# Scale and shift of the first norm as columns: stationary weight blocks against two moving columns

## The chip, the cores and the metric

One core of a Trainium2 chip. The metric is the time of the device in microseconds, the median of several executions; the profile is of one further execution.

## The reference

One layer of a trunk over 1024 latent tokens (`x`, 1024 wide) and 256 context tokens (`ctx`). What matters here is its first step: a modulated RMSNorm of both streams, whose scale and shift are products of a conditioning vector with two of the six 1024-column parts of `w_mod`.

```python
cond = jax.nn.silu(c)
cond_ctx = jax.nn.silu(c_ctx)
mod = cond @ w_mod[l] + b_mod[l]
sh1, sc1, g1, sh2, sc2, g2 = jnp.split(mod[:, None, :], N_MOD, axis=-1)
mc = cond_ctx @ w_mod[l] + b_mod[l]
csh1, csc1, cg1, csh2, csc2, cg2 = jnp.split(mc, N_MOD, axis=-1)
hc = modulate(rmsnorm(ctx, norm1_g[l]), csh1, csc1)     # h * (1 + scale) + shift
hx = modulate(rmsnorm(x, norm1_g[l]), sh1, sc1)
proj = h @ w_in
```

Before the norm a fixed position code is added to `x`. After it come the input projection, a Fourier branch and a gated recurrent branch, the output projection, a second norm, a router, and 16 experts with a SwiGLU each (the longest stage), and a last norm.

## The kernel before

All in one program; `phase_a` is the part that the change touches. Tokens are held as tiles of 128 tokens by 1024 channels (`x0` to `x7`, and `cx0`, `cx1` for the context). For the projections they are turned around: `x_tr` transposes the 128x128 block `k` of four token tiles into one 128x512 tile (PSUM), `xnT`, channels on the partitions. `make_h(k, h, ..)` then applies scale and shift per channel (`s1`, `sh1`: 128 partitions, two columns for each `k`, one for latent and one for context tokens) and splits the result into a high and a low float32r part, `hTh` and `hTl`, half `h` being tokens 0 to 511 or 512 to 1023. `proj(k, n)` multiplies these with the split weights `wh`, `wl` by three float32r matmuls each (`mm3`), into the accumulators `pj`.

*Loads.* SyncE's queue issues them in program order: eight tiles of `wmod` part 1 (the scale, `wm1_0` to `wm1_7`, 128x1024, 512 KB each), `wm0_0` of part 0 (the shift), `x0` to `x3`, then the rest of part 0 with the input weights `wr4`, `wr5` (128x512) among them, then `x4` to `x7` and the context. `x4` to `x7` reuse the buffers of `wm1_0` to `wm1_5`.

*Scale and shift (L370 to L431).* The conditioning is the stationary operand, 4 columns wide, and the rows of `wmod` move past it, 512 columns at a time. For part 1 and for `wm0_5`, `wm0_6` each tile is split into float32r parts (`m_hi` on ScalarE, `m_lo` on VectorE, 1024 columns each) and multiplied by four matmuls (`m_pe`); the other tiles of part 0 (`m_f32`) go as float32, two matmuls, but the calls after the prologue loop split `wm0_4` too. The result is two rows of 4x512. `mod_end` copies them to `modrow`, turns them with eight small transposes (`modT`, L422) and adds the bias on VectorE.

*Tokens.* `x_in(j)` adds the position code: the right half by `colpos` (on GpSimd for the tiles in `XPG`, else on VectorE), the left half by `rp`, a small matmul. `x_sq` sums squares on ScalarE, `rstd` and `norm` follow.

*Order.* A scheduler places the instructions; what is pinned (`Pinned`, `pin`) keeps the order of the program on its engine. The calls from the line with `mod_mm(1, k)` to the loop over `k` that holds `make_h` are thus an order written by hand.

The rest of the program (phases c to f and `moe`) stays as it is in the source; there GpSimd's queue loads the trig tables and the remaining parts of `wmod` (`mraw`), and VectorE sums those (`macc`, L839).

## Time and profile before

| | |
|---|---|
| median of 3 runs | 1981.69 us (1981.35 to 1982.66) |
| profiled execution | 1983.2 us |
| its span | 1981.4 us |
| TensorE busy | 1899.9 us (96%) |
| VectorE busy | 1750.4 us (88%) |
| ScalarE busy | 1357.3 us (69%) |
| GpSimd busy | 137.0 us (7%) |

The span is the profiled program from its first to its last instruction; the execution's own time is 1.8 us longer. PE is TensorE's matmuls, PEld its weight loads, DVE VectorE, ACT ScalarE, POOL GpSimd, SP SyncE. A row of the timeline gives start, duration, engine, line, operation, what is written and read, the shapes and how many instructions are merged; in brackets the idle time ahead of it and who ended it. A float32 matmul that is no transpose shows as two records. PEclk is the granted clock of TensorE as a share of 2.4 GHz.

### The profile page before, as it was taken

How to read it: one execution, taken by the hardware profiler on the slowest of the kernel's cores; microseconds unless marked ns; L12 is line 12 of the kernel's file. 1: busy time of each engine (PE TensorE's matmuls, PEld its weight loads, DVE VectorE, ACT ScalarE, POOL GpSimd, SP SyncE). 2: the span in 40 equal slices, each digit the busy share in tenths (PEclk: the TensorE clock that was granted, in tenths of full speed). 3: DMA queues.
4: the chain of work that ended last, by engine and by line, in shares of the span. 5: the costliest groups of instructions: out<-in, count | busy, mean ns of one | idle time of the engine just before them, and what ended most of it. 6: DMA issues, size and time to landing. Idle time of an engine off the chain costs nothing.

```text
span 1981.4 us, 24505 instructions
## 1 busy us (share of the span) xinstructions
PE 1899.9 (96%) x9434; PEld 1559.9 (79%) x9434; DVE 1750.4 (88%) x1629; ACT 1357.3 (69%) x1094; POOL 137.0 (7%) x134
## 2 busy tenths in 40 slices
PE   7989889969999999999999999999999999999996
PEld 2777777857787888888888888888888888888885
DVE  7889787789998989898999999998989898989897
ACT  6567643346676777777777777777777777777775
POOL 2310101220002000000000000000000000000000
PEclk9999989979999999999999999999999999999998
DMA  8353554578999999999999999999999999999994
GB/s 330 112 159 123 191 173 149 207 285 334 350 357 339 379 368 390 381 386 367 388 363 391 355 406 364 396 366 381 379 381 375 384 381 376 385 375 387 366 390 178
DMA packets 113956, 651.34 MB, mean 329 GB/s; under 512 B 12743, under 2 KB 20472, under 8 KB 46254
## 3 DMA queue, kind: packets, MB, share of 16 engines
q1 hardware_dynamic: 100718, 602.55, 79.2%
q0 software_dynamic: 10816, 38.82, 6.9%
q10 hardware_dynamic: 2304, 8.39, 1.1%
q8 instruction: 74, 1.21, 0.2%
q14 instruction: 44, 0.36, 0.0%
HBM read 622.98 MB, written 26.74 MB: 328 GB/s over the span
## 4 chain that ended last, share of the span: by engine, by line
PE 76%; DVE 9%; DMA 6%; issue 5%; ACT 1%; POOL 1%; SPq 0%; POOLq 0%; DVEq 0%; ACTq 0%
PE gu L611 44%; PE y L611 22%; PE mx L611 4%; DVE lo L228 3%; DMA mraw<-in_wmod_dram 3%; PE ht L1627 2%; DMA x<-in_x_dram 1%; DVE macc L839 1%; PE xt L1498 1%; ACT hi L227 1%; DMA trr<-in_trig_dram 1%; PE hp L1185 1%; PE pq L611 1%; DVE g L716 0%; DVE r L714 0%
## 5 line engine op out<-in xcount | busy, mean ns | idle before, releaser
L228 DVE TENSOR_TENSOR lo<-raw,hi 128x2048 fp32r<-128x2048 f32 x525 | 1197.8, 2296 | 130.2 <-ACT hi L227 128.9
L227 ACT ACTIVATE hi<-raw 128x2048 fp32r<-128x2048 f32 x525 | 1006.9, 1918 | 311.2 <-PE gu L611 210.2
L611 PE MATMUL gu<-hi,xgh 128*128 128x512 f32 (+1 forms) x1536 | 580.0, 378 | 0.0
L611 PE MATMUL gu<-hi,xgl 128*128 128x512 f32 (+1 forms) x1536 | 572.9, 373 | 0.0
L611 PE MATMUL gu<-lo,xgh 128*128 128x512 f32 (+1 forms) x1536 | 572.2, 373 | 0.0
L611 PEld LDWEIGHTS gu<-hi,xgl 128*128 128x128 f32 x1536 | 290.2, 189 | 51.8 <-DVE xgl L228 0.2
L611 PEld LDWEIGHTS gu<-lo,xgh 128*128 128x128 f32 x1536 | 290.7, 189 | 49.0 <-issue 0.2
L611 PEld LDWEIGHTS gu<-hi,xgh 128*128 128x128 f32 x1536 | 290.5, 189 | 48.6 <-issue 0.2
L611 PE MATMUL y<-hi,hh 128*128 128x512 f32 x704 | 282.3, 401 | 0.0
L611 PE MATMUL y<-hi,hl 128*128 128x512 f32 x704 | 276.2, 392 | 1.4 <-DVE hl L228 1.4
L611 PE MATMUL y<-lo,hh 128*128 128x512 f32 x704 | 275.0, 391 | 0.0
L611 PEld LDWEIGHTS y<-hi,hl 128*128 128x128 f32 x704 | 132.5, 188 | 30.7 <-DVE hl L228 1.8
L611 PEld LDWEIGHTS y<-lo,hh 128*128 128x128 f32 x704 | 132.9, 189 | 25.5 <-issue 0.2
L611 PEld LDWEIGHTS y<-hi,hh 128*128 128x128 f32 x704 | 132.8, 189 | 25.0 <-issue 0.2
L1620 ACT ACTIVATE hid<-gu 128x512 f32<-128x512 f32 x96 | 54.1, 564 | 87.1 <-PE gu L611 87.1
L1637 POOL DMA_INDIRECT accx<-ys,idx x15 | 24.0, 1598 | 1014.2 <-DVE ys L1636 940.8
L228 DVE TENSOR_TENSOR hl<-ht,hh 128x512 fp32r<-128x512 f32 x96 | 61.4, 640 | 0.0
L1621 DVE TENSOR_TENSOR hid<-hid,gu 128x512 f32<-128x512 f32 x96 | 61.0, 636 | 0.0
L1627 PE MATMUL ht<-k_ident,hid 128*128 128x128 f32 x352 | 54.7, 274 | 5.3 <-DVE hid L1621 5.3
L1627 PEld LDWEIGHTS ht<-k_ident,hid 128*128 128x128 f32 x352 | 44.1, 141 | 19.2 <-DVE hid L1621 7.3
L839 DVE SCALAR_TENSOR_TENSOR macc<-mraw,cond,macc 128x512 f32<-128x512 f32 x56 | 41.8, 748 | 18.8 <-DMA mraw<-in_wmod_dram 18.1
L227 ACT ACTIVATE hh<-ht 128x512 fp32r<-128x512 f32 x96 | 52.0, 542 | 3.5 <-PE ht L1627 3.5
(434 smaller groups left out, 1819.6 us busy)
## 6 DMA issues: line engine op xcount, KB each, us to landing
raw<-in_wg_dram SPq DMA_DIRECT2D x160, 1024.0 KB, 7.1
raw<-in_wu_dram SPq DMA_DIRECT2D x160, 1024.0 KB, 7.3
raw<-in_wd_dram SPq DMA_DIRECT2D x160, 1024.0 KB, 7.1
raw<-in_wt_dram SPq DMA_DIRECT2D x32, 1024.0 KB, 7.7
mraw<-in_wmod_dram POOLq DMA_DIRECT2D x32, 512.0 KB, 4.7
raw<-in_wdt_dram SPq DMA_DIRECT2D x16, 1024.0 KB, 6.9
wm<-in_wmod_dram SPq DMA_DIRECT2D x16, 512.0 KB, 9.7
wr<-in_win_dram SPq DMA_DIRECT2D x24, 256.0 KB, 3.5
```

The costliest lines, as they stand in the source:

```text
L227: i = self.nc.scalar.activation(hi, src, AF.Copy)
L228: j = (eng or self.nc.vector).tensor_tensor(lo, src, hi, op=ALU.subtract)
L611: i = nc.tensor.matmul(out, l, r, start=st, stop=sp)
L839: nc.vector.scalar_tensor_tensor(acc, w[:, i], c, acc, op0=ALU.mult, op1=ALU.add)
L1185: self.pin(nc.tensor.matmul(q[:, 1024:1024 + E], hT[:, k], wr[:, k], start=k == 0, stop=k == KD - 1))
L1498: nc.tensor.transpose(p[:, 128 * i:128 * i + 128], xg[:, 128 * k:128 * k + 128], self.ident)
L1620: nc.scalar.activation(hid[:, 0:w], p[:, 0, 0:w], AF.Silu)
L1621: nc.vector.tensor_tensor(hid[:, 0:w], hid[:, 0:w], p[:, 1, 0:w], op=ALU.mult)
L1627: self.nc.tensor.transpose(q[:, c:c + 128], hid[:, c:c + 128], self.ident)
L1637: self.nc.gpsimd.indirect_dma_start(out=self.accx, out_offset=bass.IndirectOffsetOnAxis(ap=idx[:, :1], axis=0), in_=ys, in_offset=None, co ...
```

## The change

The products are turned around: each 128x128 block of a `wmod` tile becomes a stationary operand and the two columns of the conditioning (`condk`, float32) move past it, so a tile takes eight float32 matmuls and the result arrives as 128 partitions with two columns per block, `modp`, to which `mod_end` adds the bias straight from PSUM. The splits of `wmod`, `modrow`, `modT` and the 4-column forms go. The first four token tiles load before `wmod`. `hTh` is computed by ScalarE straight from the normed tile with scale and shift, not from `ht`. The low parts of the input weights (`w_split`) move from GpSimd to VectorE, two of them into the loop over `k`; `x_in(4)` to `x_in(7)` all move into that loop; `colpos` of `x0` to `x4` is added on VectorE, that of `x5` to `x7` on GpSimd.

```diff
--- before.py
+++ after.py
@@ -141,9 +141,7 @@
     return out
 
 
-XPG = (0, 2, 5, 6, 7)
 PL = ((2, 0), (5, 0))
-SPL = (5, 6)
 
 
 class Pinned:
@@ -311,18 +309,15 @@
             wm[m, k] = self.c5(f"wm{m}_{k}", (128, D), tag="lr" if k < 6 else "xs") if m else self.c4(f"wm{m}_{k}")
             nc.sync.dma_start(wm[m, k], a["wmod"][m, k])
 
+        for k in range(4):
+            load_x(k)
         for k in range(KD):
             load_m(1, k)
-        load_m(0, 0)
-        for k in range(4):
-            load_x(k)
-        for k in range(1, 5):
-            load_m(0, k)
         prefetch(4, 0)
         prefetch(5, 0)
+        for k in range(KD):
+            load_m(0, k)
         prefetch(4, 1)
-        for k in range(5, KD):
-            load_m(0, k)
         prefetch(5, 1, True)
         xn = [self.c4(f"xnT{k}", (128, 2, 512)) for k in range(4)]
         xn = [xn[k // 2][:, k % 2] for k in range(KD)]
@@ -355,17 +350,14 @@
         V.tensor_scalar(self.chalf, t[4], 0.5 * LRU_C, None, op0=ALU.mult)
 
         cond = self.small("cond", 16)
-        condk = self.small("condk", 32)
-        sg = condk[:, 0:16]
+        condk = self.small("condk", 16)
+        sg = self.small("sg", 16)
         nc.scalar.activation(sg, cols[:, 0:16], AF.Sigmoid)
         nc.vector.tensor_tensor(cond, sg, cols[:, 0:16], op=ALU.mult)
         self.cond = cond
         condv = cond.rearrange("p (v k) -> p k v", v=2)
-        condk = condk.rearrange("p (k v) -> p k v", v=4)
-        V.memset(condk[:, :, 2:4], 0.0)
-        V.tensor_copy(condk[:, :, 0:2], condv)
-        cr = self.small("condr", 32, F32R).rearrange("p (k v) -> p k v", v=4)
-        self.split(condv, cr[:, :, 0:2], cr[:, :, 2:4])
+        condk = condk.rearrange("p (k v) -> p k v", v=2)
+        V.tensor_copy(condk, condv)
 
         ss, rs = self.small("ss", 10), self.small("rs", 10)
         junk = self.pro.tile([128, D], F32, tag="mraw", name="junk", bufs=2)
@@ -375,56 +367,18 @@
         def tr(name, shape=(128, 512)):
             return self.ps.tile(list(shape), F32, tag="tr", name=name, bufs=4)
 
-        modp = {}
-        PV, PA, PG = (self.pinned(e) for e in (nc.vector, nc.scalar, nc.gpsimd))
-
-        wh, wl = {}, {}
-
-        def m_hi(m, k):
-            wh[m, k] = self.c4(f"wh{m}_{k}", dt=F32R)
-            PA.activation(wh[m, k], wm[m, k], AF.Copy)
-
-        def m_lo(m, k):
-            wl[m, k] = self.c4(f"wl{m}_{k}", dt=F32R)
-            PV.tensor_tensor(wl[m, k], wm[m, k], wh[m, k], op=ALU.subtract)
-
-        def m_pe(m, k):
-            if k == 0:
-                modp[m] = [self.ps.tile([128, 512], F32, tag="pj", name=f"modp{m}{h}", bufs=4) for h in range(2)]
-            for z, w in ((0, wh), (1, wl)):
-                for h in range(2):
-                    i = nc.tensor.matmul(modp[m][h][0:4], cr[:, k], w[m, k][:, 512 * h:512 * h + 512],
-                                         start=k + z == 0, stop=k + z == KD)
-                    self.pin(i)
-
-        def m_f32(m, k):
-            if k == 0:
-                modp[m] = [self.ps.tile([128, 512], F32, tag="pj", name=f"modp{m}{h}", bufs=4) for h in range(2)]
-            for h in range(2):
-                self.pin(nc.tensor.matmul(modp[m][h][0:4], condk[:, k], wm[m, k][:, 512 * h:512 * h + 512],
-                                          start=k == 0, stop=k == KD - 1))
+        PV, PA = (self.pinned(e) for e in (nc.vector, nc.scalar))
+        modp = {m: self.ps.tile([128, KD, 2], F32, tag="pj", name=f"modp{m}", bufs=4) for m in (1, 0)}
 
         def mod_mm(m, k):
-            if m == 0 and k not in SPL:
-                return m_f32(m, k)
-            m_hi(m, k)
-            m_lo(m, k)
-            m_pe(m, k)
+            for c in range(KD):
+                self.pin(nc.tensor.matmul(modp[m][:, c], wm[m, k][:, 128 * c:128 * c + 128], condk[:, k],
+                                          start=k + c == 0, stop=k == KD - 1, skip_group_check=True))
 
         def mod_end(m):
-            c = 4
-            row = self.pro.tile([c, 1024], F32, tag="mraw", name=f"modrow{m}", bufs=2)
-            PA.activation(row[:, 0:512], modp[m][0][0:c], AF.Copy)
-            PV.tensor_copy(row[:, 512:], modp[m][1][0:c])
-            yield
-            p = tr(f"modT{m}", (128, KD, c))
-            for k in range(KD):
-                self.pin(nc.tensor.transpose(p[:, k], row[:, 128 * k:128 * k + 128], self.ident[0:c, 0:c]))
-            yield
             dv = (s1 if m else sh1).rearrange("p (k v) -> p k v", v=2)
             b = cols[:, COL["bsc"]:COL["bsc"] + 8] if m else cols[:, COL["bsh"]:COL["bsh"] + 8]
-            PV.tensor_tensor(dv, p[:, :, 0:2], b[:, :, None].to_broadcast([128, 8, 2]), op=ALU.add)
-            PV.tensor_tensor(dv, dv, p[:, :, 2:4], op=ALU.add)
+            PV.tensor_tensor(dv, modp[m], b[:, :, None].to_broadcast([128, 8, 2]), op=ALU.add)
             if m:
                 g = cols[:, COL["n1g"]:COL["n1g"] + 8]
                 PV.scalar_tensor_tensor(dv, dv, 1.0, g[:, :, None].to_broadcast([128, 8, 2]),
@@ -439,7 +393,7 @@
 
         def x_in(j, sq=True):
             p = rp.pop(j) if j in rp else x_pos(j)
-            (PG if j in XPG else PV).tensor_tensor(x[j][:, 512:], x[j][:, 512:], colpos, op=ALU.add)
+            (nc.gpsimd if j > 4 else V).tensor_tensor(x[j][:, 512:], x[j][:, 512:], colpos, op=ALU.add)
             self.pin(V.tensor_tensor(x[j][:, :512], x[j][:, :512], p, op=ALU.add))
             if sq:
                 x_sq(j)
@@ -469,33 +423,24 @@
             s = slice(512 * h, 512 * h + 512)
             t = self.pr.tile([128, 512], F32, tag="ht", name=f"ht{k}{h}", bufs=2)
             sc, sh = s1[:, 2 * k:2 * k + 1], sh1[:, 2 * k:2 * k + 1]
+            nc.scalar.activation(self.hh[k][:, s], src, AF.Identity, scale=sc, bias=sh)
             if h and k % 2:
                 nc.scalar.activation(t, src, AF.Identity, scale=sc, bias=sh)
             else:
                 V.tensor_scalar(t, src, sc, sh, op0=ALU.mult, op1=ALU.add)
-            self.split(t, self.hh[k][:, s], self.hl[k][:, s], eng=nc.gpsimd if (k, h) in PL else None)
+            (nc.gpsimd if (k, h) in PL else V).tensor_tensor(self.hl[k][:, s], t, self.hh[k][:, s], op=ALU.subtract)
 
         nc.scalar.activation(self.small("warm", 8), cols[:, COL["n1g"]:COL["n1g"] + 8], AF.Sqrt)
         for j in range(4):
             rp[j] = x_pos(j)
-        for k in range(KD):
-            mod_mm(1, k)
-        mod_mm(0, 0)
         for k in range(4):
             x_in(k)
-            if k:
-                mod_mm(0, k)
         self.rstd(ss[:, 0:4], rs[:, 0:4], 1.0 / D, self.pr, 4)
         w = {}
-        end1, end0 = mod_end(1), mod_end(0)
 
         def w_split(q):
             t, h = q % 2, q // 2
-            w[t, h] = self._get_w(4 + t, h, self.wraw.pop((4 + t, h)), True, nc.gpsimd)
-
-        for j in range(4):
-            norm(x[j], j)
-        w_split(0)
+            w[t, h] = self._get_w(4 + t, h, self.wraw.pop((4 + t, h)), True)
 
         def xn_tr(*ks):
             for k in ks:
@@ -505,33 +450,22 @@
                 else:
                     PV.tensor_copy(xn[k], p)
 
-        def m_split(k):
-            m_hi(0, k)
-            m_lo(0, k)
-
-        m_split(4)
-        xn_tr(0, 1)
-        m_split(5)
-        next(end1)
-        xn_tr(2, 3)
-        m_pe(0, 4)
+        for j in range(4):
+            norm(x[j], j)
+        for k in range(KD):
+            mod_mm(1, k)
+            if k > 5:
+                xn_tr(2 * k - 12, 2 * k - 11)
+        mod_end(1)
+        mod_mm(0, 0)
+        xn_tr(4, 5)
+        w_split(0)
+        mod_mm(0, 1)
+        xn_tr(6, 7)
         w_split(1)
-        m_split(6)
-        xn_tr(4, 5)
-        next(end1)
-        m_pe(0, 5)
-        w_split(2)
-        next(end1, None)
-        xn_tr(6, 7)
-        m_pe(0, 6)
-        x_in(4, False)
-        w_split(3)
-        mod_mm(0, 7)
-        next(end0)
-        x_sq(4)
-        x_in(5, False)
-        for _ in end0:
-            pass
+        for k in range(2, KD):
+            mod_mm(0, k)
+        mod_end(0)
         pj = {(t, n): self.ps.tile([128, 512], F32, tag="pj", name=f"pj{t}{n}", bufs=4) for t in range(2) for n in range(2)}
 
         def proj(k, n):
@@ -541,14 +475,12 @@
                 self.mm3(pj[t, n], wh[:, k % 4], wl[:, k % 4], self.hh[k][:, s], self.hl[k][:, s], k == 0, k == KD - 1)
 
         for k in range(KD):
-            if k == 2:
-                self.pin(nc.gpsimd.tensor_copy(self.small("dm", 1), cx[1][:, 0:1]))
             make_h(k, 0, xn[k])
             proj(k, 0)
-            if k == 0:
-                x_sq(5)
             if k < 2:
-                x_in(6 + k)
+                w_split(2 + k)
+            if k < 4:
+                x_in(4 + k)
             if k == 4:
                 self.rstd(ss[:, 4:8], rs[:, 4:8], 1.0 / D, self.pr, 4)
                 for j in range(4, NT):
```

TensorE, from the last tile of the scale to the first projection. `wm1_7` is the eighth tile of part 1, `tr00` a transposed block, `rp4` a position matmul, `pj00` the first projection; `x8` is eight instructions. Before:

```order
L396 MATMUL modp10_213<-wh1_7_267,condr_191 4x512
L396 MATMUL modp11_214<-wh1_7_267,condr_191 4x512
L396 MATMUL modp10_213<-wl1_7_269,condr_191 4x512
L396 MATMUL modp11_214<-wl1_7_269,condr_191 4x512
L404 MATMUL modp00_275<-wm0_0_103,condk_186 4x512
L404 MATMUL modp01_276<-wm0_0_103,condk_186 4x512
...
L437 LDWEIGHTS sel48_80
L437 MATMUL rp4_410<-enc48_79,sel48_80 128x512
L404 MATMUL modp00_275<-wm0_7_131,condk_186 4x512
L404 MATMUL modp01_276<-wm0_7_131,condk_186 4x512
...
L422 MATMUL modT0_428<-k_ident_83,modrow0_420 128x4 x8
L611 MATMUL pj00_439<-hTh0_443,wh4_0_311 128x512
```

With the change:

```order
L375 MATMUL modp1_196<-condk_186,wm1_6_107 128x2 x8
L413 MATMUL tr00_290<-k_ident_83,x0_87 128x128
...
L413 MATMUL tr10_296<-k_ident_83,x3_93 128x128
L375 MATMUL modp1_196<-condk_186,wm1_7_109 128x2 x8
L413 MATMUL tr20_310<-k_ident_83,x0_87 128x128
...
L375 MATMUL modp0_197<-condk_186,wm0_0_115 128x2 x8
L413 MATMUL tr40_332<-k_ident_83,x0_87 128x128
...
L375 MATMUL modp0_197<-condk_186,wm0_2_119 128x2 x8
...
L375 MATMUL modp0_197<-condk_186,wm0_7_129 128x2 x8
L543 MATMUL pj00_421<-hTh0_425,wh4_0_344 128x512
```

Four 512-column matmuls per tile of the scale, and two per tile of the shift, have become eight 2-column ones; the transposes stand between the tiles' blocks, `rp4` has gone behind the first projection, and the last tile's block is followed by the projection with no `modT` between.

VectorE, from the last work on the token tiles to the third `ht`. `ht00` is `ht` of block 0, first half; `wl4_1` the low part of an input weight. Before:

```order
L155 TENSOR_TENSOR x4_139<-x4_139,colpos0_85 128x512
L443 TENSOR_TENSOR x4_139<-x4_139,rp4_410 128x512
L155 COPY modrow0_420<-modp01_276 4x512
L443 TENSOR_TENSOR x5_141<-x5_141,rp5_424 128x512
L155 TENSOR_TENSOR sh1_198<-modT0_428,k_cols_77 128x16
L155 TENSOR_TENSOR sh1_198<-sh1_198,modT0_428 128x16
L475 TENSOR_SCALAR ht00_445<-xnT0_135,s1_197,sh1_198 128x512
L475 TENSOR_SCALAR ht10_463<-xnT0_135,s1_197,sh1_198 128x512
L228 TENSOR_TENSOR hTl0_444<-ht00_445,hTh0_443 128x512
L475 TENSOR_SCALAR ht20_482<-xnT1_136,s1_197,sh1_198 128x512
L228 TENSOR_TENSOR hTl1_462<-ht10_463,hTh1_461 128x512
L443 TENSOR_TENSOR x6_143<-x6_143,rp6_456 128x512
```

With the change:

```order
L226 TENSOR_TENSOR wl5_0_369<-wr5_0_113,wh5_0_368 128x512
L153 TENSOR_TENSOR sh1_195<-modp0_197,k_cols_77 128x16
L430 TENSOR_SCALAR ht00_427<-xnT0_135,s1_194,sh1_195 128x512
L396 TENSOR_TENSOR x4_139<-x4_139,colpos0_85 128x512
L431 TENSOR_TENSOR hTl0_426<-ht00_427,hTh0_425 128x512
L226 TENSOR_TENSOR wl4_1_438<-wr4_1_131,wh4_1_437 128x512
L430 TENSOR_SCALAR ht10_448<-xnT0_135,s1_194,sh1_195 128x512
L431 TENSOR_TENSOR hTl1_447<-ht10_448,hTh1_446 128x512
L397 TENSOR_TENSOR x4_139<-x4_139,rp4_441 128x512
L226 TENSOR_TENSOR wl5_1_459<-wr5_1_133,wh5_1_458 128x512
L430 TENSOR_SCALAR ht20_469<-xnT1_136,s1_194,sh1_195 128x512
L397 TENSOR_TENSOR x5_141<-x5_141,rp5_462 128x512
```

`sh1` takes one add and no `modrow` copy; the adds to `x4` and `x5` and two weight splits have moved behind it, among the `ht` and `hTl`.

## Rows read from the trace of the kernel before

**Rows 1.** Share of the span by engine, from the chain that ended last (page, part 4)

```profile
PE 76%; DVE 9%; DMA 6%; issue 5%; ACT 1%; POOL 1%; SPq 0%; POOLq 0%; DVEq 0%; ACTq 0%
```

**Rows 2.** The chain in order of time, 0 to 60 us: start us, us, what

```profile
29.87 8.37 DMA x<-in_x_dram
42.70 0.67 DVE modrow L155
44.76 1.50 DVE ht L475
46.91 2.08 PE pj L611 x4
57.23 1.23 POOL hTl L228
```

**Rows 3.** Busy time by stage: us, PE, PEld, DVE, ACT, POOL, PEclk, DMA share, GB/s

```profile
45.50:57.30 11.80, 11.12 (x32) 7.17 (x33) 7.78 (x18) 7.35 (x16) 2.15 (x4) 0.71 0.11 41
60.00:260.00 200.00, 182.91 (x885) 149.73 (x884) 167.86 (x211) 133.02 (x148) 36.61 (x55) 0.97 0.48 155
```

**Rows 4.** Timeline: first `pj`, second half's transposes (start us, us, engine, line, op, operands)

```profile
45.56 0.73 PE L611 MATMUL pj<-hTh,wh 128*128 128x512 f32 x2 [1.73 <-ACT hTh L227]
...
59.36 1.90 PEld L459 LDWEIGHTS tr<-k_ident,x 128*128 128x128 f32 x16
```

**Rows 5.** Timeline of PE, 512-column matmuls early and at 47 us; clock of that stage

```profile
15.19 1.05 PE L396 MATMUL modp<-wl,condr 128*4 128x512 f32 x2
16.05 0.66 PE L396 MATMUL modp<-wh,condr 128*4 128x512 f32 x2
...
17.01 0.62 PE L396 MATMUL modp<-wh,condr 128*4 128x512 f32 x2
17.47 0.63 PE L396 MATMUL modp<-wl,condr 128*4 128x512 f32 x2
...
47.51 0.63 PE L611 MATMUL pj<-hTh,wl 128*128 128x512 f32 x1
47.93 0.63 PE L611 MATMUL pj<-hTl,wh 128*128 128x512 f32 x1
...
47.00:48.00 1.00, 1.00 (x3) 0.81 (x4) 1.00 (x2) 0.59 (x2) 0.00 (x0) 0.50 0.00 0
```

**Rows 6.** Timeline of PE, a tile of the router's matmul among others

```profile
317.64 1.85 PE L1185 MATMUL hp-1_2617<-wrt,hT-1_2626 128*128 128x16 f32 x16
```

**Rows 7.** Router's matmul at the end of routing: PE timeline, and two stages

```profile
409.30 1.06 PE L1152 MATMUL hp<-wrt,hT 128*128 128x16 f32 x8
...
414.14 1.89 PE L1152 MATMUL hp<-wrt,hT 128*128 128x16 f32 x8 [0.69 <-ACT hT L155]
...
415.65 0.37 PE L1152 MATMUL hp<-wrt,hT 128*128 128x16 f32 x1
...
410.40:412.30 1.90, 0.00 (x0) 0.00 (x0) 1.81 (x3) 1.69 (x3) 0.00 (x0) 0.94 1.01 423
412.30:416.00 3.70, 2.98 (x12) 2.49 (x12) 3.01 (x15) 1.33 (x3) 0.13 (x1) 0.50 0.98 328
```

**Rows 8.** Timeline of ACT: starts on the landed `wm` tiles

```profile
11.85 1.06 ACT L155 ACTIVATE wh<-wm 128x1024 fp32r<-128x1024 f32 x1 [0.23 <-DMA wm<-in_wmod_dram]
13.12 1.06 ACT L155 ACTIVATE wh<-wm 128x1024 fp32r<-128x1024 f32 x1 [0.22 <-DMA wm<-in_wmod_dram]
14.41 1.06 ACT L155 ACTIVATE wh<-wm 128x1024 fp32r<-128x1024 f32 x1 [0.23 <-DMA wm<-in_wmod_dram]
```

**Rows 9.** Timeline of PE: the second `modT` half

```profile
43.43 0.40 PE L422 MATMUL modT<-k_ident,modrow 4*128 4x4 f32 x4 [0.58 <-DVE modrow L155]
```

**Rows 10.** The stage from 272 to 278 us

```profile
272.00:278.00 6.00, 6.00 (x28) 5.62 (x27) 3.46 (x7) 1.73 (x5) 0.00 (x0) 0.50 0.92 296
```

**Rows 11.** Timeline of PE: float32 transposes at either clock

```profile
32.27 1.97 PE L459 MATMUL tr<-k_ident,x 128*128 128x128 f32 x16
...
430.96 1.94 PE L1498 MATMUL xt<-k_ident,xg 128*128 128x128 f32 x8 [1.97 <-DMA xg<-hxd,idx]
```

## Prediction

> **What bounds the kernel now.** I read the share of the chain of waits first: TensorE holds 76% of it [rows 1], so a change ahead of the projections counts only by the moment at which it lets TensorE, and what follows, begin. Then the chain in order of time over the first 60 us [rows 2]: it runs through the loads of `wmod` and `x` until 38.2 us (the last starts at 29.87 and takes 8.37), then through VectorE's copy of the `modrow` half at 42.70, the first `ht` at 44.76 and the first projections (`pj`) at 46.91, on to GpSimd's `hTl` at 57.23 and the trig loads behind it on GpSimd's queue. From there the chain never goes back to a load that was issued early, and VectorE is busy 168 of the 200 us that follow 60 us [rows 3]. So I take a delay of the first `pj` (45.56 us, [rows 4]) and of the second half's transposes (59.36 us, [rows 4]) as passing to the end one for one. Third, the clock. The tables by stage print a granted clock of 1.00 from the start, yet 512-column float32r matmuls go at 0.43 us apiece until 16.0 us and at 0.23 us after it [rows 5]; 0.43 us is also the spacing in the stretch whose granted clock is 0.50. So TensorE starts at the lower level, 1.2 GHz, and rose to 2.4 GHz at 16 us, after these matmuls had followed one another since 10 us.
>
> **What goes.** The 11 pairs of high and low parts of `wmod` blocks (1.06 us on ScalarE, 1.2 us on VectorE each), the row copies and the 16 small transposes. They lie before 44 us; ScalarE and VectorE have nothing else to do there that ends later, so what they free is worth only the earlier start that the new matmuls could use. Every `hTh` now comes straight from `xnT` on ScalarE, beside `ht` instead of behind it: one `ht` (0.55 us) less in the hand-over.
>
> **What comes.** 128 float32 matmuls, each with its own 128x128 stationary block and 2 moving columns. The trace of before has no such form. The nearest is the router's matmul: a 128x128 float32 stationary block and 16 moving columns. A tile of it is 8 instructions, and the trace holds two records for each: 16 records in 1.85 us, (1.85 - 0.26) / 15 = 0.106 us apart, among other matmuls at the full clock [rows 6]; where it stands alone at the lower clock, 8 records last 1.89 us, 0.216 us apart (first start 414.14, last 415.65) [rows 7]. So 128 instructions are 256 records: 27.1 us at the full clock, 55.3 us at the lower. Even at the full clock a block of eight (1.70 us) is slower than the load that brings its data: tiles of 512 KB land 1.28 us apart (ScalarE starts on them at 11.85, 13.12 and 14.41 us, [rows 8]).
>
> A bound from below is the other small matmul, `modT`, a 4-row stationary operand and 4 moving columns: 4 records in 0.40 us, (0.40 - 0.20) / 3 = 0.07 us apart [rows 9]. It loads a sliver of the weights, so I take the router's price and keep 0.07 us (0.14 at the lower clock, by doubling) for the range.
>
> **Which clock.** This decides the sum. In the first 7 us after 13 us the old kernel's moving operand was 512 wide; the new one has nothing of that form on TensorE between 6 us and the first `pj`, only these matmuls and 32 transposes. The one place where the router's matmuls stand without 512-column matmuls around them is the end of routing: a block ran at full clock from 409.30 to 410.36, TensorE was empty until 412.3, and the granted clock then fell to 0.50 and stayed there while the next block of 8 filled 414.1 to 416.0 [rows 7]. And from 272 to 278 us TensorE was busy without a gap while the granted clock stayed at 0.50 [rows 10]. From these I take the lower level for the whole stretch, with real doubt.
>
> The Trainium skill's page "TensorE: Matmul & The Clock Gate", section "LDWEIGHTS (loading the stationary operand)", prices a load of 128 columns at 128 / 1.2 = 107 ns with no regard to the clock. The rows agree at the full clock (0.106 us) and not at the lower (0.216 us); the page's price at either clock would make the sum about that of the second case below, some 5 us later than before. I go by the rows.
>
> **Sum.** With the x tiles first, `x0` to `x3` land where `wm1_0` to `wm1_3` landed, and `wm1_0` at 13.1 us, the fifth landing [rows 8]. The x path (adds, squares, rstd, four norms, some 8 us by the rows of before) is done near 20 us and hidden; loading it first buys nothing by itself. TensorE: 13.1 + 55.3 + 32 transposes at 1.94 / 8 = 0.24 us (the lower clock, [rows 11]) = 7.8 gives 76.2. The hand-over to the first `pj` was 1.7 us (last `modT` end 43.83 to 45.56, [rows 4, 9]) through two adds, `ht` and `hTh`; now one add and `hTh`, 1.0 us. First `pj` at 77.2 against 45.56: **+31.6 us**.
>
> Then the stretch from the first `pj` to the second half's transposes, 13.8 us before. VectorE gains two weight splits (0.69 us each by `hTl`, which has the same shape), one `colpos` add and two `rp` adds (0.67 us each), 4.1 us in all; ScalarE gains two copies and two squares. VectorE was busy 7.8 of 11.8 us there [rows 3], so part fits its gaps; but `rp4` to `rp7` now sit on TensorE behind one projection each, two of them later than before. Between 0 and 4 us, I take **+2**. GpSimd loses four splits and two adds, all before 44 us, and hands on its `hTl` no earlier than its input comes. On SyncE's queue the context loads wait for the buffers of `wm1_6` and `wm1_7`, free at 13.1 + 27.6 + 2.0 = 42.7 us, and `wr6` and what follows stand behind them; the projections that use those start after 90 us in this case, so nothing is charged. Sum +33.6 on the profiled execution's 1983.2 us (span 1981.4 and 1.8 around it) is 2016.8; that execution lies 1.5 above the median of the runs, so **2015 us**. Bounds of this case: a third of the matmul stretch at the full clock, -10; records at 1.89 / 8 = 0.236 us and VectorE at its worst, +7: 2005 to 2022.
>
> **Rivals.**
> 1. *The clock rises as it did before, 6 us into the stretch.* For it: TensorE is as full as it was from 10 to 16 us, and that stream did raise it [rows 5]. Against: rows 7 and 10. Then 28 records pass in 6 us, 228 take 24.2, the transposes 1.97 / 16 x 32 = 3.9 [rows 11]: 13.1 + 6 + 24.2 + 3.9 + 1.0 = 48.2, +2.6; +2 for VectorE; and `pj` starts at the full clock, where before some 15 of its matmuls ran at 0.43 instead of 0.23 us (3 us, half of it hidden behind VectorE, -1.5). +3: 1985 us. The same page, section "Part 1: The HAM clock gate", says that the throttled clock is the default and that sustained matmul activity releases it; by that reading this case would be the likely one.
> 2. *Faster: the loads become the bound.* If a record costs what `modT`'s does and the clock is high, 256 x 0.07 + 3.9 = 21.8 us fits the loads: 16 tiles after 13.1 us at 1.28 us put `wm0_7` at 33.6, the last block ends at 34.8, `pj` starts at 35.8, 9.8 us earlier; +2 leaves -7.8: 1974 us. It decides below 1.28 / 16 = 0.08 us a record, where TensorE keeps up with the loads. Against it: every full 128x128 float32 block in the trace takes over 0.1 us.
> 3. *Cheap records at the lower clock*: 0.14 us, 13.1 + 35.8 + 7.8 + 1.0 = 57.7, +12.1 and +2: 1996 us.
>
> **How the numbers follow.** Forecast 0.62, rival 1 0.21, rival 2 0.11, rival 3 0.06. Faster by over 0.2% (4 us, about what a measurement of this kernel can tell from no change): rival 2 but for its smallest gains, 0.10. Within 0.2%: two thirds of rival 1, 0.14. Slower: the forecast, rival 3 and the rest of rival 1, 0.76. The range from 1979 to 2022 takes in the forecast with its bounds and rivals 1 and 3, and leaves out rival 2 and some tails; the forecast's own range is 2005 to 2022.
>
> **What would show it.** Right: records of the new matmul some 0.21 us apart, a granted clock of 0.50 (or matmul spacings of that level) from 13 us to the first `pj`, which begins near 77 us; the second half's transposes 32 to 36 us later than 59.4; the MoE stage unchanged in length. Rival 1: spacing of 0.106 us after the first few us and `pj` near 48. Rival 2: TensorE idle between blocks, waiting for `wm`, and `pj` near 36. I am wrong, too, if `pj` starts late but VectorE, GpSimd or the loads make it up before the MoE stage.

## The result and the profile after

The changed kernel takes **2032.9 us** (median of 4 runs, 2030.7 to 2034.1) against 1981.5 us in the same session: 1.026 times as long, 95% interval 1.0243 to 1.0276. Slower, as forecast, but 18 us above the forecast 2015 us and outside the range. The profiled execution took 2033.1 us, its span is 2031.3 us, 49.9 longer than before.

The share of the chain by engine, which answers to [rows 1], already hints at the second half of the story: TensorE has 81% of a longer span.

```profile
PE 81%; DVE 9%; DMA 5%; issue 3%; ACT 2%; POOL 0%; SPq 0%; POOLq 0%; DVEq 0%; ACTq 0%
```

The chain in order of time (start us, us, what) answers to [rows 2]: from 13 us to the trig loads near 94 us no load stands in it; the new matmuls stand there instead.

```profile
13.01 24.03 PE modp L375 x112
...
53.89 20.29 PE modp L375 x96
75.27 3.01 PE pj L543 x6
93.95 3.02 DMA trr<-in_trig_dram
```

PE's timeline of the start (start us, us, engine, line, operation, operands; answers to [rows 4, 5, 11]). 112 records in 24.03 us are (24.03 - 0.35) / 111 = 0.213 us apart, and TensorE does nothing else from 13.01 us to the end of the last block at 74.2 us than these and 32 transposes. The first `pj` starts at 75.27 us, 29.7 later than before; the spacing of 512-column matmuls falls from 0.43 to 0.23 us at 79.6 us; the second half's transposes start at 91.14 us, 31.6 later than before (59.59 us on PE; the 59.36 of [rows 4] is their first weight load).

```profile
13.01 24.03 PE L375 MATMUL modp<-condk,wm 128*128 128x2 f32 x112 [7.10 <-DVE sp L343]
36.90 1.95 PE L413 MATMUL tr<-k_ident,x 128*128 128x128 f32 x8
...
75.27 1.22 PE L543 MATMUL pj<-hTh,wh 128*128 128x512 f32 x2 [1.11 <-ACT hTh L426]
...
77.23 0.63 PE L543 MATMUL pj<-hTl,wh 128*128 128x512 f32 x1
77.66 0.63 PE L543 MATMUL pj<-hTh,wl 128*128 128x512 f32 x1
...
79.60 0.40 PE L543 MATMUL pj<-hTl,wh 128*128 128x512 f32 x1
79.83 0.39 PE L543 MATMUL pj<-hTh,wl 128*128 128x512 f32 x1
...
91.14 1.02 PE L413 MATMUL tr<-k_ident,x 128*128 128x128 f32 x7
```

The stretch that answers to [rows 3] (us, PE, PEld, DVE, ACT, POOL, clock, DMA share, GB/s). The printed 1.00 at the low clock is the value ahead of the first recorded change, as before.

```profile
75.20:91.20 16.00, 15.07 (x49) 9.05 (x50) 12.83 (x27) 12.54 (x22) 3.40 (x3) 1.00 0.20 56
```

At the last `pj` (83.29 us before, 111.75 now) the delay is 28.5 us, and at the first `gu` matmul of the expert stage (432.7 us before, 461.1 now) it is 28.4 us. That is what a delayed start should look like. Then the expert stage itself grew. There each piece of the streamed weights (128x2048, 1 MB) lands in `raw`, is split into `hi` and `lo` (four buffers in turn, `hi0` to `hi3`), and moves as 512 columns past a stationary block: of the gathered tokens (`xgh`, `xgl`) for `gu`, of the hidden values (`hh`, `hl`) for `y`. Two groups of its `gu` matmuls, by tile (ns min/median/max, then first and last start in us), before and after:

```profile
L611 PE MATMUL gu<-hi,xgh x1536: 277/389/799, 432.7 to 1952.2; 128*128 128x512 f32 x160, 128*128 128x256 f32 x32
L611 PE MATMUL gu<-hi,xgl x1536: 278/389/628, 433.8 to 1952.4; 128*128 128x512 f32 x160, 128*128 128x256 f32 x32
```

```profile
L543 PE MATMUL gu<-hi,xgh x1536: 277/392/794, 461.1 to 2003.6; 128*128 128x512 f32 x160, 128*128 128x256 f32 x32
L543 PE MATMUL gu<-hi,xgl x1536: 278/394/628, 462.1 to 2003.9; 128*128 128x512 f32 x160, 128*128 128x256 f32 x32
```

The second group goes from 1518.6 us to 1541.8 us, first start to last: **+23.2 us**, with the median of one matmul at 394 instead of 389 ns. 28.4 and 23.2, less 1.7 in the tail, are the 49.9. The clock does not explain it: its granted share over 1520 us of the stage rounds to 1.00 in both traces (from 433 us before, from 460 us after). The instructions of TensorE, ScalarE and VectorE stand in the same order, and a split lasts what it did (1.92 us on ScalarE, 2.30 us on VectorE, in both). The matmuls are simply further apart. Taken by the piece of weights that they read, from the first start to the last of each piece, they take 23.8 us more in sum up to the last `y`, while the time between pieces shrinks by 2.5 us; the pieces that go as 256-column matmuls take the same within 0.1 us. The first and last of the twelve `gu` matmuls that read `hi2` and `lo2`, at the same place before and after: (895.97 - 893.48) / 11 = 0.2264 us, and (927.28 - 924.71) / 11 = 0.2336 us.

```profile
893.48 0.39 PE L611 MATMUL gu<-hi,xgh 128*128 128x512 f32 x1
...
895.97 0.39 PE L611 MATMUL gu<-hi,xgl 128*128 128x512 f32 x1
```

```profile
924.71 0.40 PE L543 MATMUL gu<-hi,xgh 128*128 128x512 f32 x1
...
927.28 0.39 PE L543 MATMUL gu<-hi,xgl 128*128 128x512 f32 x1
```

### The profile page after: what moved, and what is told of

Its sections match the earlier page's. It is cut to its first block, busy times and chain, and to the rows that moved or that the text cites. A ratio compares the mean times of both kernels' runs of the same rounds, so it can differ in the third digit from the quotient of the medians.

```text
span 2031.3 us, 24815 instructions
## 1 busy us (share of the span) xinstructions
PE 1954.9 (96%) x9610; PEld 1607.2 (79%) x9610; DVE 1737.3 (86%) x1618; ACT 1347.1 (66%) x1080; POOL 127.5 (6%) x127
## 4 chain that ended last, share of the span: by engine, by line
PE 81%; DVE 9%; DMA 5%; issue 3%; ACT 2%; POOL 0%; SPq 0%; POOLq 0%; DVEq 0%; ACTq 0%
PE gu L543 45%; PE y L543 23%; PE mx L543 4%; DMA mraw<-in_wmod_dram 3%; PE modp L375 3%; DVE lo L226 2%; PE ht L1559 2%; DVE macc L771 1%; PE xt L1430 1%; PE hp L1117 1%; DMA trr<-in_trig_dram 1%; DVE g L648 1%; DVE r L646 0%; DVE r L645 0%; DMA xg<-hxd,idx 0%
## 5 line engine op out<-in xcount | busy, mean ns | idle before, releaser
L375 PE MATMUL modp<-condk,wm 128*128 128x2 f32 x256 | 54.7, 350 | 7.1 <-DVE sp L343 7.1
L375 PEld LDWEIGHTS modp<-condk,wm 128*128 128x128 f32 x256 | 55.2, 333 | 8.0 <-DVE sp L343 8.0
```

Of the source, the lines that this page charges most:

```text
L375: self.pin(nc.tensor.matmul(modp[m][:, c], wm[m, k][:, 128 * c:128 * c + 128], condk[:, k], start=k + c == 0, stop=k == KD - 1, skip_group ...
```

## Experiments on the expert stage: where the tiles lie

The change drops two small tiles of the constant pool, `condr` (32 float32, 128 bytes per partition) and `dm` (it takes 32 bytes), and makes two 64-byte tiles of one of 128. The weight pool behind it begins with a padding tile of 32 elements (`PAD`); so `raw`, `hi0` to `hi2` and `lo0` to `lo2` moved down by 160 bytes, while `hi3`, `lo3`, `xgh`, `xgl`, `hh` and `hl`, which lie in a pool filled from the other end, stayed. In the built programs `hi0` begins at byte 103840 before and 103680 after; `xgh` at 157600, `hi3` at 173984 in both. Before, all the tiles named here begin at the remainder 416 by 512 bytes; after, the moved ones begin at 256. **Theory 1**: this costs the 23 us. **Theory 2**: the late start, the loads or the clock do. A kernel for which no interval is given, here and below, ran once; executions of the kernel before lay between 1976 and 1986 us.

**a_pad72 and b_pad120**: one number changed, in the changed kernel so that the tiles are back, in the kernel before so that they lie as after the change by 512 bytes.

```diff
-    PAD = 32
+    PAD = 72
```

```diff
-    PAD = 32
+    PAD = 120
```

> The changed kernel with the padding tile of the expert stage 40 elements (160 bytes) per partition longer, so that the streamed weight tiles hi0 to hi2 and lo0 to lo2 lie at the same addresses as in the kernel before; nothing else differs. Theory 1 (the place of these tiles in the on-chip memory makes the expert stage's matmuls slower): from the first to the last gu matmul the time falls from about 1543 us back to about 1520 us, the spacing of gu matmuls on tiles hi0 to hi2 from 0.234 to 0.2264 us, and the kernel takes about 2010 us. Theory 2 (the slower expert stage comes from the shifted start, the loads or the clock): the expert stage stays at 1543 us and the kernel at about 2033 us.

> The kernel before with the padding tile of the expert stage 88 elements (352 bytes) per partition longer, which puts hi0 to hi2 and lo0 to lo2 at the same remainder by 512 bytes as in the changed kernel. Theory 1: the expert stage gets some 21 to 23 us longer, spacing 0.234 us on hi0 to hi2 and 0.230 on hi3, and the kernel takes about 2003 us. Theory 2: nothing changes, 1981.5 us.

```profile
L543 PE MATMUL gu<-hi,xgl x1536: 278/389/628, 461.1 to 1978.1; 128*128 128x512 f32 x160, 128*128 128x256 f32 x32
```

```profile
L611 PE MATMUL gu<-hi,xgl x1536: 278/394/628, 435.2 to 1976.9; 128*128 128x512 f32 x160, 128*128 128x256 f32 x32
```

The same group of each: 1517.0 us in a_pad72, 1541.7 us in b_pad120. The kernels took 2009.4 us (1.0157 times the kernel before, 1.014 to 1.0174) and 2006.9 us (1.0142, 1.0125 to 1.0159). Theory 1 holds in both directions: 160 bytes of padding are worth 23 us of the changed kernel, and 352 bytes cost the kernel before as much in this stage. Its whole time grew by 28 us, of which the trace places 23 in the stage; the rest is of the order by which executions of the kernel before differed in that session (5 us).

**b_pad40 and b_pad48** ask which distance counts (PAD = 40 and 48 in the kernel before, 32 and 64 bytes further).

> The kernel before with the padding tile 8 elements (32 bytes) longer, so that the moved tiles lie at a remainder of 0 by 64 bytes, while the tiles that stay lie at 32. Theory 1a (the remainder by 64 bytes decides): about 2003 us, as with the changed kernel. Theory 1b (the remainder by 512 bytes decides): some other time, between 1975 and 2010 us. Theory 2: 1981.5 us.

> The kernel before with the padding tile 16 elements (64 bytes) longer: the moved tiles keep their remainder of 32 by 64 bytes and have another one by 512. Theory 1a (the remainder by 64 bytes decides): 1981.5 us and gu spacing 0.2264 us. Theory 1b (the remainder by 512 bytes decides): slower, 1985 to 2005 us. Theory 2: 1981.5 us.

```profile
L611 PE MATMUL gu<-hi,xgl x1536: 277/393/628, 431.2 to 1969.3; 128*128 128x512 f32 x160, 128*128 128x256 f32 x32
```

```profile
L611 PE MATMUL gu<-hi,xgl x1536: 279/392/628, 434.3 to 1958.9; 128*128 128x512 f32 x160, 128*128 128x256 f32 x32
```

1538.1 us and 1524.6 us (kernels 1998.6 and 1989.7 us): 32 bytes cost 19.5 us, near the 23 of 160 and 352, 64 bytes 6.0. So theory 1a missed at 64 bytes, where it had 1981.5 us and the old spacing; theory 1b, the remainder by 512, takes in both times, but with wide ranges.

**a_padhl** leaves `raw` where the change put it and moves only `hi0` to `hi2` and `lo0` to `lo2` back (`self.ma.tile([128, 40], F32, name="pad2")` behind the ten `raw` tiles). **a_padmo** leaves all these where the change put them and moves the other pool's tiles by the same 160 bytes (`self.mo.tile([128, 40], F32, name="pad3")` behind `onesm`).

> The changed kernel with 160 bytes of padding per partition between the raw weight tiles, which stay at their shifted addresses, and hi0 to hi2 and lo0 to lo2, which come back to those of the kernel before. Theory 1 (TensorE's reads of hi and lo, or the writes that make them, depend on the address): expert stage back at about 1519 us, kernel about 2010 us. Theory 2 (the writes of the loads into the raw tiles, or their reads by ScalarE and VectorE, depend on it): expert stage stays near 1543 us, kernel about 2033 us. In between if both count.

> The changed kernel with 160 bytes of padding at the other end, so that hi3, lo3, the gathered tokens' high and low parts and the hidden tiles move down by the same 160 bytes as hi0 to hi2 and lo0 to lo2 did: all of them lie as to one another as in the kernel before, at another address. Theory 1 (where tiles lie as to one another decides): expert stage back at about 1520 us, kernel about 2010 us. Theory 2 (each tile's own address by 64 or 512 bytes decides): expert stage at 1543 us or more, hi3 too at 0.2336 us, kernel 2033 to 2045 us.

```profile
L543 PE MATMUL gu<-hi,xgl x1536: 279/389/632, 462.4 to 1979.6; 128*128 128x512 f32 x160, 128*128 128x256 f32 x32
```

```profile
L543 PE MATMUL gu<-hi,xgl x1536: 278/389/628, 464.3 to 1980.3; 128*128 128x512 f32 x160, 128*128 128x256 f32 x32
```

1517.2 us and 1516.0 us, kernels 2010.4 and 2011.0 us: both full recoveries. So the loads' writes into `raw` don't matter, and the moved address is not bad by itself. What counts is how `hi` and `lo` lie to something in the other pool.

**a_padx and b_padx** find the partner: 160 bytes that move `xg`, `xgh` and `xgl` alone, in the changed kernel towards `hi0` to `hi2`, in the kernel before away from every `hi`.

```diff
             mo.tile([128, KD, 128], F32R, tag="xgl", name="z_xgl", bufs=2)
+            mo.tile([128, 40], F32, name="pad4")
```

> The changed kernel with 160 bytes of padding that moves only the gathered tokens (xg, xgh and xgl, the stationary operands of gu), so that they lie to hi0 to hi2 as in the kernel before, but no longer to hi3; the hidden tiles hh and hl (the stationary operands of y) stay. Theory A (the moving against the stationary operand of the same matmul): spacing of gu back to 0.2264 us on hi0 to hi2 and up to 0.2336 on hi3, y still slow on hi0 to hi2 (0.2336 to 0.2345 us), kernel about 2018 us. Theory B (a tile being read against one being written by the other engines, among hi and lo): spacings stay at 0.234 on hi0 to hi2 and 0.230 on hi3, kernel about 2033 us.

> The kernel before with the same 160 bytes, so that xg, xgh and xgl alone leave their place relative to all of hi and lo. Theory A: gu at 0.2336 us or near it on all four tiles, y unchanged at 0.2291 us, kernel about 2000 us. Theory B: nothing changes, about 1980 us.

One group of `gu` and one of `y` by shape (count, busy us, mean ns): before, after, a_padx, b_padx, in this order.

```profile
L611 PE MATMUL gu<-hi,xgl 128*128 128x512 f32 x1280 | 500.4, 391 | 0.0
...
L611 PE MATMUL y<-lo,hh 128*128 128x512 f32 x704 | 275.0, 391 | 0.0
```

```profile
L543 PE MATMUL gu<-hi,xgl 128*128 128x512 f32 x1280 | 506.3, 396 | 0.0
...
L543 PE MATMUL y<-lo,hh 128*128 128x512 f32 x704 | 277.4, 394 | 0.0
```

```profile
L543 PE MATMUL gu<-hi,xgl 128*128 128x512 f32 x1280 | 503.3, 393 | 0.0
...
L543 PE MATMUL y<-lo,hh 128*128 128x512 f32 x704 | 278.6, 396 | 0.0
```

```profile
L611 PE MATMUL gu<-hi,xgl 128*128 128x512 f32 x1280 | 507.2, 396 | 0.0
...
L611 PE MATMUL y<-lo,hh 128*128 128x512 f32 x704 | 275.8, 392 | 0.0
```

In b_padx `gu` is as slow as it ever was and `y`, whose stationary operands did not move, stays near its old 391 ns; in a_padx `gu` is half mended and `y` is not. By buffer, the middle value over all groups of twelve matmuls (last start less first start, by 11, in us; the starts are read to 0.01 us, so a value is good to 0.001):

| | `gu` on hi0 / hi1 / hi2 / hi3 | `y` on hi0 / hi1 / hi2 / hi3 |
|---|---|---|
| before | 0.2264 / 0.2264 / 0.2264 / 0.2264 | 0.2291 / 0.2291 / 0.2291 / 0.2291 |
| after | 0.2345 / 0.2336 / 0.2336 / 0.2300 | 0.2345 / 0.2336 / 0.2336 / 0.2309 |
| a_padx | 0.2291 / 0.2273 / 0.2273 / 0.2336 | 0.2345 / 0.2336 / 0.2336 / 0.2309 |
| b_padx | 0.2345 / 0.2345 / 0.2345 / 0.2345 | 0.2300 / 0.2300 / 0.2309 / 0.2300 |
| b_pad48 | 0.2309 / 0.2291 / 0.2291 / 0.2309 | 0.2336 / 0.2291 / 0.2300 / 0.2309 |

This is theory A: the matmul is slower where its moving and its stationary operand do not lie to one another as in the kernel before. In a_padx `hi3` got slow as A had it, and `hi0` to `hi2` came back, `hi0` not quite (A had 0.2264 for all three). In sums over all groups, against the kernel before: after, `gu` on `hi0` to `hi3` takes 6.2, 5.1, 5.1 and 0.7 us more; in a_padx 1.6, 0.5, 0.5 and 5.5; in b_padx 5.2 to 5.9 on each, and `y` 0.3 on each. The kernels took 2022.1 us (2018 expected) and 2003.2 us (2000). Theory B, a clash with tiles that the other engines write, would have left `gu` in b_padx alone, so it is not the cause.

It may add a small part. `hi3` is half a step slower in the changed kernel (0.2300) and in b_pad48 (0.2309), though it and `xgh` had not moved, which A does not explain; nor does it explain `hi0` in a_padx. In all three cases ScalarE was filling a buffer at another remainder while TensorE read this one (in these traces it fills `hi2` while TensorE reads `hi3`, and `hi3` while TensorE reads `hi0`); at 64 bytes this part is as large as the main one. No run separates the two, and which part of the memory or of TensorE makes the main difference was not tried.

## Experiments on the start: the clock

These keep the tiles at the old addresses, so they compare with a_pad72 (2009.4 us, first `pj` at 74.5 us).

**a_warm and a_warm2** put 18 unused bf16 matmuls of 512 columns between the position matmuls and the first scale block, with 48 rows (a_warm, shown) or, the operands' other rows filled with ones, 128 rows (a_warm2):

```diff
         for j in range(4):
             rp[j] = x_pos(j)
+        dum = self.ps.tile([128, 512], F32, tag="pj", name="dum", bufs=4)
+        def dummy():
+            self.pin(nc.tensor.matmul(dum, sel48[:, 0], enc48, start=True, stop=True))
+        for j in range(18):
+            dummy()
```

> The changed kernel with the expert stage's tiles at the old addresses, and 18 extra bf16 matmuls of 512 columns (their result is not used) between the four position matmuls and the first scale matmul, so that TensorE is densely busy from 4 us to the first scale tile. Theory 1 (the stream of fp32 weight blocks with two moving columns neither raises the clock nor keeps it): a few records at 0.106 us after 13 us, then 0.215 us again, and the kernel within 5 us of the 2009 us of the same kernel without the extra matmuls. Theory 2 (it keeps a clock that is up): records at 0.106 us to the end of the stream, first pj near 45 us, about 1979 us. Theory 3 (the price belongs to the fp32 weight load and not to the clock): 0.215 us from the start, 2009 us.

> As the kernel with 18 extra matmuls ahead of the scale, which went at 0.44 us each to their end without the clock rising, but with 128 rows in them instead of 48 (ones in the rows that were not there). Theory 1 (how many of the array's rows work decides whether a stream counts, and the blocks with two moving columns count too little): the extra matmuls go from 0.43 to 0.22 us each before 13 us, then the records of scale and shift start at 0.106 us and fall back to 0.215 us within the stream, first pj between 60 and 74 us. Theory 2 (a raised clock stays through the stream): records at 0.106 us throughout, first pj near 45 us, about 1979 us. Theory 3 (the price is the weight load's own at either clock): 0.215 us from the first record, about 2007 us. Theory 4 (rows do not matter): the extra matmuls stay at 0.43 us and the kernel at 2007 us.

PE's timeline, a_warm and then a_warm2, and two windows of a_warm2:

```profile
5.86 7.88 PE L439 MATMUL dum<-enc,sel 48*128 48x512 bf16 x18
13.68 24.05 PE L375 MATMUL modp<-condk,wm 128*128 128x2 f32 x112
```

```profile
7.45 6.56 PE L442 MATMUL dum<-enc,sel 128*128 128x512 bf16 x18
...
13.92 4.26 PE L378 MATMUL modp<-condk,wm 128*128 128x2 f32 x37
...
21.74 4.41 PE L378 MATMUL modp<-condk,wm 128*128 128x2 f32 x20
...
14.00:18.00 4.00, 4.00 (x38) 4.00 (x37) 3.15 (x14) 2.52 (x6) 0.00 (x0) 1.00 1.03 418
22.00:26.00 4.00, 4.00 (x20) 4.00 (x21) 0.00 (x0) 0.00 (x0) 0.00 (x0) 0.50 1.03 404
```

In a_warm TensorE was busy without a gap from 4.2 to 13.7 us, and the clock did not rise: (7.88 - 0.61) / 17 = 0.43 us a matmul to the end. The records stand 0.213 us apart from the first, as its theory 3 had it; but with no raised clock to keep, none of its theories was put to the test. In a_warm2 the clock rose on the way (18 in 6.56 us), and here the same blocks show both prices: 37 records in 4.26 us, 0.11 us apart, at a granted clock of 1.00, and 20 in 4.41 us, 0.213 us apart, at 0.50. The clock fell near 19 us, inside the stream of blocks, and did not come back until after the first `pj` (71.2 us). So a clock raised beforehand was not kept: the outcome of a_warm2's theory 1. That the number of rows made it rise, and not the ones in them, no run separates. Its 3.3 us at the first `pj` were lost again on the way (`mx` starts at 312.9 us, in a_pad72 at 311.4), and the kernel took 2010.5 us; a_warm took 2007.3 us.

**a_mix2 and a_mixw** also put one such matmul behind every second fp32 matmul of scale and shift (48 and 128 rows).

```diff
                                           start=k + c == 0, stop=k == KD - 1, skip_group_check=True))
+                if c % 2 == 1:
+                    dummy()
```

> As the kernel with the 18 extra matmuls, and one more such matmul of 512 columns after every second fp32 matmul of scale and shift (64 of them). Theory 1 (wide matmuls between the blocks hold the clock): records at 0.106 us, extra matmuls some 0.22 us each, so the stream takes 128 x 0.212 + 64 x 0.22 = 41 us instead of 54, the transposes half their time, first pj near 60 us and about 1993 us. Theory 2 (the clock falls all the same): records at 0.215 us and 64 x 0.43 = 28 us more than without, about 2037 us. Theory 3 (the price belongs to the fp32 weight load): 0.215 us with extra matmuls at 0.22 us, about 2023 us.

> As the kernel with the 128-row extra matmuls ahead, and one more of them after every second fp32 matmul. Theory 1 (wide matmuls with all rows hold the clock): records at 0.106 us, extra matmuls at 0.22 us or a little more, a pair with its extra matmul in 0.65 to 0.75 us instead of 1.48, first pj near 60 us, about 1993 us. Theory 2 (the clock falls all the same): 1.48 us each as with 48 rows, about 2047 us. Theory 3 (the blocks' price stands at either clock): 0.86 + 0.22 = 1.1 us each, about 2023 us.

```profile
20.85 1.01 PE L375 MATMUL modp<-condk,wm 128*128 128x2 f32 x4
21.79 0.61 PE L441 MATMUL dum<-enc,sel 48*128 48x512 bf16 x1
22.33 1.01 PE L375 MATMUL modp<-condk,wm 128*128 128x2 f32 x4
```

```profile
20.39 0.50 PE L378 MATMUL modp<-condk,wm 128*128 128x2 f32 x4
20.75 0.38 PE L444 MATMUL dum<-enc,sel 128*128 128x512 bf16 x1
20.96 0.50 PE L378 MATMUL modp<-condk,wm 128*128 128x2 f32 x4
...
47.47 0.85 PE L378 MATMUL modp<-condk,wm 128*128 128x2 f32 x4 [0.24 <-issue]
48.18 0.59 PE L444 MATMUL dum<-enc,sel 128*128 128x512 bf16 x1
48.56 0.85 PE L378 MATMUL modp<-condk,wm 128*128 128x2 f32 x4
...
14.00:46.00 32.00, 31.62 (x275) 30.44 (x280) 10.53 (x24) 6.10 (x12) 4.14 (x3) 1.00 0.94 367
47.00:60.00 13.00, 12.52 (x60) 11.92 (x62) 0.00 (x0) 0.00 (x0) 0.00 (x0) 0.50 0.00 1
```

With 48 rows a pair and its extra matmul take 1.48 us throughout and the kernel 2048.9 us, 12 more than its theory 2 had; with 128 rows 0.57 us (20.39 to 20.96), the kernel 1992.6 us and the first `pj` starts at 62.6 us. Work that is thrown away saves 17 us. But at 46.3 us the clock fell here too, with the same mixture on TensorE, and rose again near 67 us; why it held for 32 us and then not stays open. The 1993 us of theory 1 were met partly by luck: its rounds were cheaper than forecast (0.57 us for 0.65 to 0.75), and the fall took that back. Nor is the whole gap between the two kernels the clock: with 128 rows a round at the granted clock of 0.50 takes 1.09 us (47.47 to 48.56), not 1.48, with the records 0.213 us apart in both. The extra matmul's weight load starts together with the record ahead of it there (50.16 us), and with 48 rows 0.28 us after it (21.51 and 21.79 us).

## Experiments on the start: the orientation

**a_rows** takes a_pad72 and gives scale and shift their old form back (`m_hi`, `m_lo`, `m_pe`, `m_f32`, `modrow` and `modT` as before, now in the changed kernel's order), keeping its loads and its direct `hTh`. **a_rows2** also moves the fifth token tile's position add:

```diff
-            (nc.gpsimd if j > 4 else V).tensor_tensor(x[j][:, 512:], x[j][:, 512:], colpos, op=ALU.add)
+            (nc.gpsimd if j > 3 else V).tensor_tensor(x[j][:, 512:], x[j][:, 512:], colpos, op=ALU.add)
```

> The changed kernel with its order of loads, its direct first-half hTh and its other moves kept, but scale and shift computed as in the kernel before (two or four moving-side rows: the condition is the stationary operand and the weights stream past in matmuls of 512 columns, split in high and low parts for the scale, plain fp32 for most of the shift, then row copies and small transposes), and with the expert stage's weight tiles at the addresses of the kernel before. Theory (the orientation with stationary weight blocks costs the start all that was lost there): the first pj starts near 44 us instead of 74.5 and the kernel takes 1975 to 1982 us, no more than the kernel before. Rival (the other moves, such as the pinned order or the fifth to eighth token tiles' late work, cost part of it): the first pj starts near 44 us but the kernel stays above 1985 us, or the first pj starts after 50 us.

> As the kernel with the old orientation restored, but the position add of the fifth token tile runs on GpSimd, so that VectorE, which stood 9.7 us before it for that tile's load, goes on with the low parts of the scale weights. Theory (that wait alone kept the first pj from 45 to 51 us): the first pj starts near 51 us instead of 59.0 and the kernel takes 1982 to 1988 us. Rival (behind that wait stands another, a buffer or a load): the first pj starts after 55 us and the kernel stays above 1989 us.

a_rows (timeline of DVE and of PE), then a_rows2 (PE):

```profile
35.98 0.69 DVE L437 TENSOR_TENSOR x<-x,colpos 128x512 f32<-128x512 f32 x1 [9.71 <-DMA x<-in_x_dram]
...
38.45 1.01 PE L391 MATMUL modp<-wl,condr 128*4 128x512 f32 x2 [7.46 <-DVE wl L154]
...
59.02 0.73 PE L588 MATMUL pj<-hTh,wh 128*128 128x512 f32 x2 [1.32 <-ACT hTh L467]
```

```profile
17.92 1.02 PE L391 MATMUL modp<-wh,condr 128*4 128x512 f32 x2 [12.05 <-ACT wh L154]
...
50.57 0.73 PE L588 MATMUL pj<-hTh,wh 128*128 128x512 f32 x2 [1.32 <-ACT hTh L467]
```

In a_rows the rival of its expectation came: VectorE stood 9.7 us before an add for a tile still on its way, with the low parts of the last scale block queued behind it, and TensorE 7.5 us behind those (first `pj` 59.0 us, 1992.9 us, 1.0042 to 1.0087 times the kernel before). With the add elsewhere the first `pj` is at 50.6 us and the kernel at 1985.4 us (1.0023, 1.0012 to 1.0033). Against a_pad72 that is 23.9 us at the first `pj` and 23.9 us at the end (25.4 when each is taken against the kernel before of its own session): the price of the orientation, but for the one add that a_rows2 moves besides. The other 5.0 us (50.57 against 45.56) go with the new order, by the trace with the loads': the first scale matmul starts at 17.9 instead of 8.2 us, its splits behind squares and norms on ScalarE, and the clock is raised later. No run has the old order of loads alone. No version here beats the kernel before.

## Why the prediction was wrong

**The step that failed** is the expert stage's own length. The sum let a delay of the first `pj` pass "to the end one for one" and gave the stage no term of its own; "the MoE stage unchanged in length" was named as a sign of being right, and no row stood for it. The delay itself passed nearly one for one: 29.7 us at the first `pj`, 28.5 at the last, 28.4 at the first `gu`. But the stage got 23.2 us longer, because the tiles that the change dropped moved three of the four buffers of its moving operand by 160 bytes, and its stationary ones not. With the tiles put back the kernel takes 2009.4 us, inside the forecast's own range (2005 to 2022), 5.6 below its number.

**Price and clock**: right. 0.213 us a record against 0.216, TensorE full from 13.0 to 74.2 us, and the clock low until after the first `pj`. The Trainium skill's page "TensorE: Matmul & The Clock Gate", section "LDWEIGHTS (loading the stationary operand)", gives 107 ns for 128 columns and names no clock; a_warm2 has 0.11 and 0.213 us for the same blocks, so the measurement agrees at the full clock and decides against it at the lower. **Rival 1**, that the clock rises some us into the stream, fell twice: it did not rise in 61 us, and where it had been raised it fell. The same page of the Trainium skill, section "Part 1: The HAM clock gate", by which sustained matmul activity releases the clock, would have made it the likely one; 61 us of gapless matmuls did not release it here. **Rivals 2 and 3** had no ground, since the records cost what the router's did.

**First `pj`**: 77.2 forecast, 75.27 measured: 1.4 us less in the records and 0.6 in the transposes. **The 2 us for VectorE**: the stretch from the first `pj` to the second half's transposes did grow, by 1.8 us (14.0 to 15.9, both ends taken on PE), but 49 matmuls lie in it instead of 38; to the last `pj` it is 1.3 us shorter. The low clock also ended 4.3 us after the first `pj`, where before it had lasted 7.9 us. So the term met its number at that point, but not for VectorE's work alone. In all it is +28.4 us where +33.6 was forecast: the sum's own error is 5 us to the high side, and it hid a fifth of the 23: without the expert stage the forecast would have been right, and a little high.

## What to carry to other kernels

When a change adds or drops a tile of any size, list the start of every large tile before and after, and keep the moving and the stationary operands of the long matmul stages at their old distance with padding; otherwise 160 bytes in a prologue can cost nearly as much as the work that it changes (23 us beside 28 here). Price small fp32 matmuls with a stationary block each by the block, at the clock that their own stream has in the trace, not at the clock of their neighbours. And read a forecast of "the rest is unchanged" as a claim that needs a row of its own.

## What was not expected of the hardware

- 512-column float32r matmuls 0.2264 us apart where `hi` and `xgh` lie at the distance of the kernel before; 0.2291 to 0.2309 us at 64 bytes from it; 0.2336 to 0.2345 us at 32, 160 and 352 bytes from it. That is some 3% a matmul, and 1.5% of the stage (23 of 1519 us).
- 22 bf16 matmuls of 512 columns with 48 rows (4 of the position code and 18 extra), without a gap from 4.2 to 13.7 us, left the clock low (a_warm); with 128 rows in the 18, the other rows ones, it rose (a_warm2).
- With the fp32 records 0.213 us apart, a round of two blocks and one 512-column bf16 matmul took 1.09 us with 128 rows in the latter (a_mixw) and 1.48 us with 48 rows (a_mix2).
- 61 us of gapless fp32 blocks with two moving columns passed at the lower clock, and in a_warm2 the clock, up at 13.9 us, was down again near 19 us under such a stream.
